# A hybrid recurrence block on one Trainium2 core: w_out by seven products of halves, and the first layer norm's gamma and beta on turned tokens

## The chip, the cores and the metric

The kernel runs on one core of one Trainium2 chip. TensorE (PE) multiplies and transposes into PSUM, VectorE (DVE) and ScalarE (ACT) work on tiles of SBUF and PSUM, GpSimd (POOL) does small things, and SyncE (SP), ScalarE and GpSimd each have a queue on which they issue DMAs. The metric is the device time of one execution in microseconds (us), the median of several runs.

## The reference

One decoder block over 1024 tokens with 1024 channels, all float32:

```
proj = x @ w_in  -> q, f, i, og, pool_v, gate_a, gate_b      (each 1024 wide)
o = HGRN2(q, f, i)                  # gated recurrence, 8 heads of 128
a = rmsnorm_per_head(o) * g * sigmoid(og) @ w_a
b = (causal_mean(pool_v) - pool_v) @ w_pool * pool_scale     # 4 groups, windows 2, 4, 8, 16
mix = (sigmoid(gate_a) * a + sigmoid(gate_b) * b) @ w_out
x = LN1(alpha * x + mix)            # gain ln1_g, bias ln1_b
x = LN2(alpha * x + relu(x @ w_up)^2 @ w_down)               # hidden width 4096
```

## The kernel before

**Products in three parts.** A float32 operand is split into a high half (rounded to the fp32r format, a cast on ScalarE) and a low half (operand minus high half, a subtraction on VectorE). One 128-deep step of a product is three matmuls of 128x512: high by high, high by low, low by high. A tile with two halves of 512 columns comes from the pool `act`; the parts of a weight tile come from the ring `w` (`w_part`, L256 and L257; `NW` = 10 tiles, so five pairs).

**Products by halves.** Most large products (w_in, w_a, w_up, w_down) are already done by seven products of halves in place of eight: tokens and weights are each cut into four quarters a11, a12, a21, a22 and b11 ... b22, sums of quarters are formed (on tokens s1 ... s4, on weights t1 ... t4), and seven products of such quarters are added up with signs. `pair` writes the seven out for two columns of blocks, `prod` (L219, L221, L222) issues one of them: four 128-deep steps, twelve matmuls. Its results leave PSUM by a copy on ScalarE (L303) and additions on VectorE (L307). The product by w_out alone is done whole: `mix(t, cc)` takes a row of 128 tokens and 512 columns and runs `mm3` (L114 to L116) over eight steps, 24 matmuls, in 16 such groups.

**Order.** A scheduler places each engine's instructions by the priority of the code's order and its own clock; `tc.high_priority` and `tc.issue_after` bend it. Nothing overtakes on an engine or a DMA queue at run time.

**The stretch in question.** Around 640 us the products by w_a end; `gated` multiplies by the gates (`ga`, from DRAM) and adds the pooled branch (`gb`), and the result is split and kept as `merged[u][j]` (u: half of the tokens, j: block of 128 channels). Then come the w_out groups. After each, `scalar_tensor_tensor` adds alpha times the residual into the row tile `r[t]` (L1390), `bn_stats` takes the statistics, and after a row's second half `layer_norm` runs: a square root on ScalarE (L1339), an Identity with scale and bias (L1350), a product by gamma on VectorE (L1351) and an addition of beta on POOL (L1352); rows 6 and 7 do it all on VectorE in halves. The finished row goes to DRAM (`xd`, issued on SP) for the second residual, and is transposed on TensorE into turned tokens (channels on partitions), rows 0 to 3 by `first_tokens` (a11, a12) and rows 4 to 7 by `second_tokens` (s3 and a22; s2, s1, s4 follow from them). When the left halves of rows 4 to 7 have been transposed, blocks of w_up for the third pair of units are loaded into their tiles (`r<-in_w_up_dram`, SP). `units(i, raw)` is one pair of blocks of the up stage, i from 0 to 15: product by w_up, Relu, Square (L1434, L1435), sums, and stores of hidden tiles (`put`).

**Pools.** All tiles of SBUF come from rings; an operation that wants a tile of a ring waits until the one that it replaces has been read. `act` has 28, `rows` 8, `c` (from `ca`, `wq` and, in the up stage, `up`) 4, 2 and 4.

## Time and profile before

| | us |
|---|---|
| median of 3 runs (lowest, highest) | 1435.21 (1435.06, 1435.75) |
| the profiled execution | 1434.66 |
| its span, from first to last instruction | 1433.0 |
| TensorE busy | 1420.8 |
| VectorE busy | 1099.2 |
| ScalarE busy | 753.2 |
| POOL busy | 110.9 |

The mean granted TensorE clock was 0.999 of full speed. A busy share is an average over stages with different limits, and matmuls overlap each other, so that the distance from one's start to the next one's start says what it costs. In a row of a timeline, the last bracket is the engine's idle time before the instruction and what ended it.

### The profile page before, as it was taken

How to read it: one execution, taken by the hardware profiler on the slowest of the kernel's cores; microseconds unless marked ns; L12 is line 12 of the kernel's file. 1: busy time of each engine (PE TensorE's matmuls, PEld its weight loads, DVE VectorE, ACT ScalarE, POOL GpSimd, SP SyncE). 2: the span in 40 equal slices, each digit the busy share in tenths (PEclk: the TensorE clock that was granted, in tenths of full speed). 3: DMA queues.
4: the chain of work that ended last, by engine and by line, in shares of the span. 5: the costliest groups of instructions: out<-in, count | busy, mean ns of one | idle time of the engine just before them, and what ended most of it. 6: DMA issues, size and time to landing. Idle time of an engine off the chain costs nothing.

```text
span 1433.0 us, 21208 instructions
## 1 busy us (share of the span) xinstructions
PE 1420.8 (99%) x7499; PEld 1180.1 (82%) x7499; DVE 1099.2 (77%) x1832; ACT 753.2 (53%) x1376; POOL 110.9 (8%) x300
## 2 busy tenths in 40 slices
PE   9999999999999999999999999999999999999997
PEld 7888888888888888878888888888888888888886
DVE  6967887897797796679965697666666887777978
ACT  5445566566656656455522376555556433433534
POOL 0002011111212110100003000000000100000000
PEclk9999999999999999999999999999999999999999
DMA  7142254444444546899551315444457864444422
GB/s 272 60 140 89 90 131 148 126 115 150 113 118 133 150 123 190 237 322 340 182 198 74 103 59 188 153 159 161 162 177 243 299 235 146 150 151 157 132 74 118
DMA packets 187179, 228.18 MB, mean 159 GB/s; under 512 B 12576, under 2 KB 111168, under 8 KB 187072
## 3 DMA queue, kind: packets, MB, share of 16 engines
q1 hardware_dynamic: 180464, 210.94, 44.6%
q0 software_dynamic: 5824, 13.63, 4.7%
q10 hardware_dynamic: 784, 2.25, 0.5%
q8 instruction: 59, 0.97, 0.3%
q14 instruction: 48, 0.39, 0.1%
HBM read 149.70 MB, written 77.07 MB: 158 GB/s over the span
## 4 chain that ended last, share of the span: by engine, by line
PE 95%; DVE 2%; DMA 1%; ACT 1%; issue 1%; POOL 0%; DVEq 0%; ACTq 0%; SPq 0%; POOLq 0%
PE ps_pj L219 16%; PE ps_pj L222 16%; PE ps_pj L221 16%; PE ps_pj L1565 4%; PE ps_pj L1566 4%; PE ps_pj L1564 4%; PE ps_pj L115 2%; PE ps_pj L114 2%; PE ps_pj L116 2%; PE ps_tr L1566 2%; PE ps_tr L1565 2%; PE ps_tr L1564 2%; PE ps_hg L219 1%; PE ps_sc L219 1%; PE ps_sc L222 1%; PE ps_hg L221 1%
## 5 line engine op out<-in xcount | busy, mean ns | idle before, releaser
L219 PE MATMUL ps_pj<-act,w 128*128 128x512 f32 x1068 | 419.9, 393 | 0.3 <-ACT c L303 0.2
L222 PE MATMUL ps_pj<-act,w 128*128 128x512 f32 x1068 | 415.3, 390 | 0.0
L221 PE MATMUL ps_pj<-act,w 128*128 128x512 f32 x1068 | 415.3, 389 | 0.0
L256 ACT CAST w<-raw 128x512 fp32r<-128x512 f32 x303 | 187.7, 621 | 255.4 <-PE ps_pj L221 169.7
L257 DVE TENSOR_TENSOR w<-raw,w 128x512 fp32r<-128x512 f32 x303 | 207.2, 686 | 93.6 <-ACT w L256 92.3
L219 PEld LDWEIGHTS ps_pj<-act,w 128*128 128x128 f32 x1068 | 200.5, 188 | 44.1 <-ACT c L303 1.3
L222 PEld LDWEIGHTS ps_pj<-act,w 128*128 128x128 f32 x1068 | 200.5, 188 | 42.4
L221 PEld LDWEIGHTS ps_pj<-act,w 128*128 128x128 f32 x1068 | 200.6, 188 | 40.5
L1526 ACT CAST act<-act 128x1024 fp32r<-128x1024 f32 x66 | 67.0, 1050 | 108.2 <-issue 35.0
L1527 DVE TENSOR_TENSOR act<-act,act 128x1024 fp32r<-128x1024 f32 x66 | 79.4, 1220 | 18.1 <-ACT act L1526 18.1
L1566 PE MATMUL ps_pj<-act,act 128*128 128x512 f32 x240 | 93.0, 389 | 0.0
L1565 PE MATMUL ps_pj<-act,act 128*128 128x512 f32 x240 | 93.0, 389 | 0.0
L1564 PE MATMUL ps_pj<-act,act 128*128 128x512 f32 x240 | 92.5, 389 | 0.0
L307 DVE TENSOR_TENSOR c<-c,ps_pj 128x512 f32<-128x512 f32 x91 | 62.1, 682 | 32.5 <-PE ps_pj L222 31.8
L303 ACT COPY c<-ps_pj 128x512 f32<-128x512 f32 x92 | 53.3, 581 | 3.0 <-PE ps_pj L222 1.9
L1564 PEld LDWEIGHTS ps_pj<-act,act 128*128 128x128 f32 x240 | 45.0, 188 | 9.4
L1565 PEld LDWEIGHTS ps_pj<-act,act 128*128 128x128 f32 x240 | 45.0, 188 | 9.4
L1566 PEld LDWEIGHTS ps_pj<-act,act 128*128 128x128 f32 x240 | 45.0, 188 | 9.3
L312 DVE TENSOR_TENSOR raw<-raw,raw 128x512 f32<-128x512 f32 x43 | 29.6, 689 | 25.5 <-DMA raw<-in_w_in_dram 16.1
L1435 ACT ACTIVATE c<-c 128x512 f32<-128x512 f32 x61 | 38.5, 632 | 1.7
L1434 ACT ACTIVATE c<-c 128x512 f32<-128x512 f32 x46 | 29.0, 632 | 16.4 <-DVE c L307 16.4
L751 POOL DMA_DIRECT2D s<-og x28 | 24.9, 1161 | 133.2 <-DVE og L1177 133.2
(433 smaller groups left out, 2684.6 us busy)
## 6 DMA issues: line engine op xcount, KB each, us to landing
h<-c SPq DMA_DIRECT2D x106, 256.0 KB, 3.0
raw<-in_w_in_dram SPq DMA_DIRECT2D x100, 256.0 KB, 3.3
act<-h SPq DMA_DIRECT2D x78, 256.0 KB, 3.0
draw<-in_w_down_dram SPq DMA_DIRECT2D x16, 1024.0 KB, 8.2
raw<-in_w_up_dram SPq DMA_DIRECT2D x56, 256.0 KB, 2.9
hf<-h SPq DMA_DIRECT2D x34, 256.0 KB, 3.0
s<-og POOLq DMA_DIRECT2D x28, 256.0 KB, 6.4
v<-v SPq DMA_DIRECT2D x16, 256.0 KB, 3.5
```

The source lines that it names most:

```text
L219: PE.matmul(ps, wh[:, k], th, start=first and k == 0, stop=False, skip_group_check=True)
L221: PE.matmul(ps, wh[:, k], tl, start=False, stop=False, skip_group_check=True)
L222: PE.matmul(ps, wl[:, k], th, start=False, stop=k == CH - 1, skip_group_check=True)
L256: hi_of.append(A.copy(hi, src).ins)
L257: lo_of.append(V.tensor_sub(lo, src, f(hi)).ins)
L303: noted(A.copy(t, ps))
L307: last_add[0] = V.tensor_add(t, t, ps).ins
L1526: A.copy(hi, src)
L1527: V.tensor_sub(lo, src, f(hi))
L1564: PE.matmul(ps, hh[:, w], wh, start=fresh and n == 0, stop=False, skip_group_check=True)
L1565: PE.matmul(ps, hh[:, w], wl, start=False, stop=False, skip_group_check=True)
L1566: PE.matmul(ps, hl[:, w], wh, start=False, stop=n == M - 1, skip_group_check=True)
```

## The change

**The w_out product** becomes seven products of quarters, by `out_product`: p1, p2, p6, p5, p3, p7, p4, each of four groups of twelve matmuls, which go on in two chains of four PSUM banks. Each product's result is added into the rows by `scalar_tensor_tensor` as it comes. The sums of w_out's quarters (t1 to t4) are formed early, before the recurrence, by `out_sums`: loads into tiles that the recurrence uses later, four operations on VectorE for each k, and stores to DRAM on POOL's queue. The operands are split when they are needed: `split_tokens` for the gated rows, `split_rows` (loads on POOL's queue into `c` tiles) for the weights.

**The first layer norm.** Rows 0 to 3 get their sums from `accum_out` and a Square on ScalarE, rows 4 to 7 keep `bn_stats`. `norm_row` writes only the normalised row, without gain and bias, and stores it (`nd`). Gain and bias go on behind the transposes, where they are one number per partition: in `first_normed` for rows 0 to 3, and by an Identity in `second_tokens(normal=True)` for rows 4 to 7. `prm` holds them; two more small loads are issued on ScalarE's queue at the start.

**The residual rows** with gain and bias, for the second layer norm, are made in the up stage, one row after each of `units` 5 to 12: `residual_row` loads `nd` on POOL's queue into one of three `y` tiles, does four operations on VectorE, and stores `xd` on POOL's queue. The pool for w_down's blocks (`fw`) opens later for it.

```diff
+        def out_sums(k, queue, *tags):
+            rooms = [tt(tag) for tag in tags]
+            for t, (kh, nh) in zip(rooms, ((0, 1), (1, 1), (0, 0), (1, 0))):
+                queue.dma_start(out=t, in_=out_rows_of(kh, nh)[k])
+            b12, b22, b11, b21 = rooms
+            V.tensor_sub(b22, b22, b12)
+            V.tensor_sub(b12, b12, b11)
+            V.tensor_add(b11, b22, b11)
+            V.tensor_sub(b21, b21, b11)
+            for name, t in (("t3", b22), ("t1", b12), ("t2", b11), ("t4", b21)):
+                nc.gpsimd.dma_start(out=out_td[name][k], in_=t)
...
+        for k in range(CH):
+            out_sums(k, nc.gpsimd if k > 1 else nc.sync, *(("tA", "tA", "tE", "tD") if k % 2 else ("tH", "tH", "st", "st")))
...
+        def split_tokens(srcs):
+            return [split_act(t) for t in srcs]
+
+        def split_rows(srcs, tile_of):
+            made = []
+            for src in srcs:
+                t, (hi, lo) = c_tile(), tile_of()
+                nc.gpsimd.dma_start(out=t, in_=src)
+                A.copy(hi, t)
+                V.tensor_sub(lo, t, f(hi))
+                made.append((hi, lo))
+            return made
...
+    def out_product(name, chain, fresh, u, nh, whole, then=None):
...
+            ps, w = chains[chain][c], slice(c * P, (c + 1) * P)
+            for k, ((xh, xl), (wh, wl)) in enumerate(zip(xs, ws)):
+                PE.matmul(ps, xh[:, w], wh, start=fresh and k == 0, stop=False, skip_group_check=True)
+                PE.matmul(ps, xh[:, w], wl, start=False, stop=False, skip_group_check=True)
+                PE.matmul(ps, xl[:, w], wh, start=False, stop=k == CH - 1, skip_group_check=True)
...
+            with tc.high_priority(PRIO):
+                if whole and u:
+                    V.scalar_tensor_tensor(y, y, scale, ps, ALU.mult, ALU.add)
+                    V.bn_stats(parts_of_row[t][:, nh], y)
...
+        for i in range(2 if t == 7 else 1):
+            w = slice(i * HALF, (i + 1) * HALF) if t == 7 else slice(0, D)
+            A.activation(y[:, w], y[:, w], AF.Identity, bias=mv[:, 2:3], scale=mv[:, 3:4])
+            nc.sync.dma_start(out=nd[t][:, w], in_=y[:, w])
...
+    out_product("p1", 1, True, 0, 0, False)
+    out_ops["p2"].insert(0, split_tokens(tokens(0, 1)))
+    out_ops["p6"] = split_tokens(s2), split_rows(out_td["t2"], row_parts)
+    out_product("p2", 0, True, 0, 0, True)
...
+    out_product("p3", 1, False, 0, 1, True, norm_row)
+    out_ops["p4"] = split_tokens(tokens(1, 1)), split_rows(out_td["t4"], act_parts)
+    out_product("p7", 0, True, 1, 1, True)
+    xt[:] = [r[c][:, HALF:] for c in range(CH)], [c_tile() for _ in range(CH)], [r[c][:, :HALF] for c in range(CH)]
+    first_normed("a12", "pj")
+    first_normed("a11", "pj")
+    out_product("p4", 0, False, 1, 0, True, norm_row)
...
+                if normal:
+                    t = s[kp] if name == "s3" else half_act()
+                    normed(t, ps, kp + CH * (name == "a22"))
+                    ps = t
...
+        def residual_row(t):
+            y = res.tile([P, D], F32, tag="y", name=nm("y"), bufs=3)
+            nc.gpsimd.dma_start(out=y, in_=nd[t])
+            for i in range(2):
+                w = slice(i * HALF, (i + 1) * HALF)
+                V.tensor_mul(y[:, w], y[:, w], g1[:, w])
+                V.tensor_add(y[:, w], y[:, w], b1[:, w])
+            nc.gpsimd.dma_start(out=xd[t], in_=y)
...
             run(units(i, raw))
+            if 0 <= i - 5 < 8:
+                residual_row(i - 5)
```

Where the instructions stand shows in the built order. First, ScalarE at the turn from the w_out stage into the up stage, before. The first two rows are the statistics of rows 6 and 7 (r_1639 and r_1644, which VectorE normalises); r_1629 is the tile of row 4, and the cast from it takes a block of w_up that has been loaded there:

```order
L1339 ACTIVATE lmv_1643_8771<-lmv_1643_8771,eps_ln_88 128x1
L1339 ACTIVATE lmv_1648_8837<-lmv_1648_8837,eps_ln_88 128x1
L256 CAST w_1671_8940<-raw_1654_8860 128x512
L256 CAST w_1675_8959<-raw_1655_8862 128x512
L256 CAST w_1678_8977<-raw_1651_8855 128x512
L303 COPY c_1662_8898<-ps_pj_1661_8885 128x512
L256 CAST w_1681_8983<-raw_1680_8981 128x512
L1434 ACTIVATE c_1662_8898<-c_1662_8898 128x512
L256 CAST w_1695_9059<-r_1629_8582 128x512
L132 CAST act_1664_8906<-r_1593_8246 128x512
```

The same place after, with r_1620, r_1622, r_1624 and r_1626 the tiles of rows 4, 5, 6 and 7, L1443 the Identity of `norm_row`, L273 what was L256:

```order
L1443 ACTIVATE r_1620_8461<-r_1620_8461,lmv_1688_8907 128x1024
L1438 ACTIVATE lmv_1689_8928<-lmv_1689_8928,eps_ln_88 128x1
L273 CAST w_1724_9119<-raw_1723_9117 128x512
L1438 ACTIVATE lmv_1690_8949<-lmv_1690_8949,eps_ln_88 128x1
L273 CAST w_1740_9201<-r_1620_8461 128x512
L320 COPY c_1705_9030<-ps_pj_1704_9017 128x512
L1443 ACTIVATE r_1622_8477<-r_1622_8477,lmv_1689_8928 128x1024
L1438 ACTIVATE lmv_1691_8970<-lmv_1691_8970,eps_ln_88 128x1
L1443 ACTIVATE r_1624_8493<-r_1624_8493,lmv_1690_8949 128x1024
L1501 ACTIVATE c_1705_9030<-c_1705_9030 128x512
L1443 ACTIVATE r_1626_8509<-r_1626_8509,lmv_1691_8970 128x512 x2
```

The cast from row 4's tile stood behind the normalisation of all eight rows; now it stands behind row 4's and ahead of that of rows 5, 6 and 7. Second, TensorE at the same place, before (r_1629, r_1634, r_1639, r_1644 are rows 4 to 7):

```order
L222 MATMUL ps_pj_1661_8885<-act_1620_8542,w_1660_8882 128x512
L177 MATMUL ps_tr_1663_8900<-ident_74,r_1629_8582 128x128
L177 MATMUL ps_tr_1663_8900<-ident_74,r_1634_8648 128x128
L177 MATMUL ps_tr_1663_8900<-ident_74,r_1639_8714 128x128
L177 MATMUL ps_hg_1665_8909<-ident_74,r_1629_8582 128x128
```

and after, from the last transposes of row 5 on:

```order
L177 MATMUL ps_tr_1710_9052<-ident_74,r_1622_8477 128x128
L177 MATMUL ps_sc_1712_9062<-ident_74,r_1622_8477 128x128
L177 MATMUL ps_tr_1706_9032<-ident_74,r_1624_8493 128x128
L177 MATMUL ps_hg_1708_9042<-ident_74,r_1624_8493 128x128
L177 MATMUL ps_tr_1710_9052<-ident_74,r_1624_8493 128x128
L177 MATMUL ps_sc_1712_9062<-ident_74,r_1624_8493 128x128
L177 MATMUL ps_tr_1706_9032<-ident_74,r_1626_8509 128x128
L177 MATMUL ps_hg_1708_9042<-ident_74,r_1626_8509 128x128
L177 MATMUL ps_tr_1710_9052<-ident_74,r_1626_8509 128x128
L177 MATMUL ps_sc_1712_9062<-ident_74,r_1626_8509 128x128
L236 MATMUL ps_pj_1716_9080<-act_1681_8862,w_1714_9076 128x512
```

Before, three rows are transposed together, and the fourth behind them. After, the transposes go row by row: row 4's four, then twelve products less four that stand between them, then rows 5, 6 and 7, and behind these 24 products by parts (w_1714 first) that are made earlier. Third, VectorE in the up stage, where before the parts of w_up and the additions follow each other:

```order
L257 TENSOR_TENSOR w_1796_9647<-raw_1786_9604,w_1795_9646 128x512
L257 TENSOR_TENSOR w_1799_9665<-raw_1785_9603,w_1798_9664 128x512
L344 TENSOR_TENSOR raw_1785_9603<-raw_1787_9606,raw_1786_9604 128x512
L307 TENSOR_TENSOR c_1772_9524<-c_1772_9524,ps_pj_1761_9452 128x512
L257 TENSOR_TENSOR w_1803_9688<-raw_1785_9603,w_1802_9687 128x512
```

and after, where y_1886, y_1916 and y_1946 are the first three residual rows, and L274 is what was L257:

```order
L274 TENSOR_TENSOR w_1838_9772<-raw_1829_9745,w_1837_9771 128x512
L1566 TENSOR_TENSOR y_1886_10063<-y_1886_10063,ln_1797_9579 128x512 x2
L354 TENSOR_TENSOR raw_1829_9745<-raw_1829_9745,raw_1831_9748 128x512
L1567 TENSOR_TENSOR y_1886_10063<-y_1886_10063,ln_1798_9581 128x512 x2
L324 TENSOR_TENSOR c_1817_9668<-c_1817_9668,ps_pj_1806_9596 128x512
L274 TENSOR_TENSOR w_1841_9791<-raw_1831_9748,w_1840_9790 128x512
L1566 TENSOR_TENSOR y_1916_10230<-y_1916_10230,ln_1797_9579 128x512 x2
L274 TENSOR_TENSOR w_1844_9809<-raw_1830_9747,w_1843_9808 128x512
L1567 TENSOR_TENSOR y_1916_10230<-y_1916_10230,ln_1798_9581 128x512
L1566 TENSOR_TENSOR y_1946_10397<-y_1946_10397,ln_1797_9579 128x512
```

The code asks for a residual row after each of units 5 to 12; in the order all eight stand in one run of 66 operations, of which 32 are theirs, from the parts of unit 4 on.

217 lines of the change are left out of this document (113 added, 104 removed).

## The prediction

> **What bounds the kernel now.** I read the page first, then the waits of TensorE, then its timeline for the pitch of the products, then sums by stretch around the place of the change, and last the single rows there. The page's head, its chain and the waits of TensorE (engine, line, for whom, us in total, times, longest):
>
> ```profile
> span 1433.0 us, 21208 instructions
> PE 1420.8 (99%) x7499; PEld 1180.1 (82%) x7499; DVE 1099.2 (77%) x1832; ACT 753.2 (53%) x1376; POOL 110.9 (8%) x300
> PE 95%; DVE 2%; DMA 1%; ACT 1%; issue 1%; POOL 0%; DVEq 0%; ACTq 0%; SPq 0%; POOLq 0%
> PE ps_hg L480 <- POOL ident masks.py:199: 1.8, 1, 1.8
> PE ps_tr L114 <- DVE f L905: 1.4, 1, 1.4
> PE ps_tr L177 <- DVE x L204: 0.7, 1, 0.7
> PE ps_sc L538 <- DVE c L580: 0.5, 1, 0.5
> PE ps_pj L219 <- ACT c L303: 0.2, 1, 0.2
> ```
>
> TensorE carries 95% of the chain and waits 4.6 us in all (1.8 + 1.4 + 0.7 + 0.5 + 0.2). So two things alone move the time: fewer products, or a new wait on TensorE. Taking work off another engine earns nothing. What a product is worth comes from the timeline (start, length, engine, line), in the middle of the w_out stage:
>
> ```profile
> 760.16 0.39 PE L115 MATMUL ps_pj<-w,act 128*128 128x512 f32 x1
> 760.39 0.39 PE L116 MATMUL ps_pj<-w,act 128*128 128x512 f32 x1
> 760.62 0.39 PE L114 MATMUL ps_pj<-act,act 128*128 128x512 f32 x1
> 760.84 0.39 PE L115 MATMUL ps_pj<-act,act 128*128 128x512 f32 x1
> ```
>
> Each row is 0.39 us long, but starts come 0.227 us apart (three steps in 0.68): the pitch is the price, not the length. Now the sums by stretch (us from:to, length, busy us of PE, PEld, DVE, ACT, POOL, clock):
>
> ```profile
> 100.00:120.00 20.00, 20.00 (x90) 16.57 (x89) 12.34 (x19) 10.12 (x18) 0.00 (x0) 1.00 0.26 80
> 640.00:710.00 70.00, 70.00 (x310) 57.96 (x309) 67.75 (x112) 41.13 (x75) 0.00 (x0) 1.00 0.84 277
> 720.00:810.00 90.00, 90.00 (x414) 74.60 (x414) 52.90 (x91) 27.60 (x45) 14.39 (x6) 1.00 0.32 116
> 820.00:830.00 10.00, 10.00 (x49) 8.27 (x49) 9.27 (x17) 6.35 (x12) 0.00 (x0) 1.00 0.44 134
> 830.00:870.00 40.00, 39.78 (x180) 32.69 (x179) 40.00 (x68) 29.36 (x53) 0.00 (x0) 1.00 0.34 114
> 900.00:1000.00 100.00, 100.00 (x443) 82.81 (x442) 61.83 (x95) 56.66 (x96) 0.00 (x0) 1.00 0.46 156
> ```
>
> VectorE is packed ahead of the w_out stage (67.75 of 70), half idle within it (52.90 of 90), and without a gap from 830 to 870, in the first units of the up stage. There TensorE keeps running by a hair. The change puts work into the idle part, and its end touches the packed part.
>
> **1. Fewer products.** Out go 16 groups of 24 products (384); in come seven of 48 (336). 48 x 0.227 = 10.9 us of TensorE. The rest of TensorE's list is as long as before: 6149 rows become 6101. Term: -10.9.
>
> **2. VectorE inside the w_out stage.** Its unit price is the step between back-to-back operations:
>
> ```profile
> 842.01 2.49 DVE L206 TENSOR_TENSOR c<-r,c 128x512 f32<-128x512 f32 x4
> 844.42 1.28 DVE L257 TENSOR_TENSOR w<-raw,w 128x512 fp32r<-128x512 f32 x2
> L1351 DVE TENSOR_TENSOR r<-r,act 128x1024 f32<-128x1024 f32 x6 | 7.4, 1226 | 7.0 <-ACT r L1350 7.0
> ```
>
> Four in 2.41 us: 0.60 each. The stage gets 24 more low halves (56 for 32), 12 more additions into the rows (28 for 16) and 16 sums of token tiles, and loses 8 bn_stats: 44 x 0.60 = 26.4. The six gamma products (7.4) go. That is +19.0, and idle are 90 - 52.90 = 37.1, less the 10.9 by which the stage shrinks: some 7 us are left over. What VectorE loses by standing behind a late load must fit in there. Where it has always work it is idle 3% (640 to 710) to 7% (820 to 830): 2.5 to 5.8 of 79 us, both under 7. Each product's operands are needed one by one, so I take +0.5, with 0 to 5 as bounds (5 if it idles 15%, 12 us).
>
> **3. The turn into the up stage.** Here a wait is added, and it is the dearest item. Before, rows 4 to 7 are all normalised before any engine waits for the w_up block that is loaded into their left halves:
>
> ```profile
> 818.37 0.49 PE L177 MATMUL ps_sc<-ident,r 128*128 128x128 f32 x3
> 821.88 0.62 ACT L256 CAST w<-r 128x512 fp32r<-128x512 f32 x1 [1.57 <-DMA r<-in_w_up_dram]
> 822.40 0.62 ACT L132 CAST act<-r 128x512 fp32r<-128x512 f32 x1
> 822.93 0.63 ACT L1435 ACTIVATE c<-c 128x512 f32<-128x512 f32 x1
> 823.46 0.57 ACT L303 COPY c<-ps_pj 128x512 f32<-128x512 f32 x1
> 823.92 1.66 ACT L132 CAST act<-r 128x512 fp32r<-128x512 f32 x3
> L1350 ACT ACTIVATE r<-r,lmv 128x1024 f32<-128x1024 f32 x6 | 7.5, 1246 | 2.5 <-DVE lmv L1349 2.5
> r<-in_w_up_dram SPq DMA_DIRECT2D x4, 256.0 KB, 3.8
> x<-r SPq DMA_DIRECT2D x7, 512.0 KB, 2.6
> ```
>
> From the end of the transposes that free the tile (818.37 + 0.49) to the cast that waited for the load are 3.0 us; the wait is ScalarE's alone and TensorE runs on. In the new order the same cast (of row 4's tile) stands on ScalarE ahead of the normalisation of rows 5, 6 and 7, whose transposes stand on TensorE ahead of 24 products that are ready. So TensorE waits for: the load (3.0), the cast (0.52, by the starts above), a copy (0.46), row 5 (1.2), row 6 (1.2), two small square roots (0.2 together), a Relu (0.53) and the halves of row 7 (1.06): 8.2. It has 8 products left to do in that time, 1.8 us. Term: +6.4. Low end 2 (the load lands while ScalarE is still at the statistics of these rows, and the four normalisations alone are late); high end 9.8 (the store of row 4 must land first, 2.6 us, and the load takes its 3.8). I take 6.4, by the row that is the same load into the same tile.
>
> The Trainium skill, DMA: Bandwidth & Descriptors, section "Anatomy of one DMA", fits 2.0 us plus bytes over 436 GB/s, an estimate of 2.6 us for these 256 KB, for transfers issued from GpSimd; by it the wait would be 6.0 and the time 0.4 lower. This case's row, 3.8 on SP's queue, says rather longer.
>
> **4. Gamma and beta on turned tokens.** Eight Identity operations on ScalarE take the place of eight copies; eight more (0.53 each) stand before the s3 and a22 operands, in the packed stretch, where TensorE's wait at L219 was 0.2. Most of them run while TensorE works on a11 and a12: +0.3, bounds 0 and 4.2 (all eight in the way).
>
> **5. The sums of w_out before the recurrence.** 16 VectorE operations (9.6 us) go into stretches like 100 to 120, idle 7.7 of 20, so there is room for them; but the order puts them ahead of the recurrence's first scan. At worst about half of them, 5 us, push that scan back. Against that:
>
> ```profile
> 132.15 0.75 DVE L1072 TENSOR_TENSOR tC<-tE,ek 128x256 f32<-128x256 f32 x2
> 135.80 0.60 PE L1092 MATMUL ps_tr<-ident,tC 128*128 128x128 f32 x4
> ```
>
> The scan's result is ready at 132.90 and TensorE takes it at 135.80: 2.9 us of cover. +0.3, bounds 0 and 2.1 (5 less 2.9).
>
> **6. Residual rows in the up stage.** 32 operations, 19.2 us, where VectorE is idle 38 of 100. But the order packs all eight rows into one run of 66 operations (39.6 us) that holds 14 low halves of w_up parts; one such part feeds 12 products, so TensorE needs 14 x 12 x 0.227 = 38.1 us for them. The three y tiles go round: a tile's store and the next load must land before the fourth row.
>
> ```profile
> act<-x POOLq DMA_DIRECT2D x7, 512.0 KB, 7.2
> s<-og POOLq DMA_DIRECT2D x28, 256.0 KB, 6.4
> s<-og SPq DMA_DIRECT2D x16, 256.0 KB, 2.5
> c<-o POOLq DMA_DIRECT2D x8, 256.0 KB, 5.3
> ```
>
> A turn is 6.4 + 7.2 = 13.6 us by these, against 14 operations (8.4) between the first row's end and the fourth's start: 5.2 of standing; later rows add 1.0 and 1.8. With the 1.5 by which 39.6 exceeds 38.1, VectorE falls 9.5 behind. The parts run ahead by up to four pairs of w tiles, 4 x 12 x 0.227 = 10.9, or by three PSUM banks, 8.2. So 0 to 1.3: +0.5; if the cover is gone, up to 4.
>
> The two loads that ScalarE issues more at the start lie beside TensorE's longest wait, for POOL: nothing. POOL's six additions (14.39 us) go, off the path: nothing.
>
> **The sum.** -10.9 + 0.5 + 6.4 + 0.3 + 0.3 + 0.5 = -2.9. The profiled execution took 1434.66 us (its span and 1.7 around it), so 1431.8; the median of the three runs was 1435.21, 0.55 above it, so 1432.3. 0.2% is 2.9 us, about what a measurement of this kernel can tell from no change; the forecast lies on that line.
>
> **Rivals.**
> A: the wait at the turn is covered (the load lands before ScalarE gets to it, VectorE being the later). Then -10.9 and about 1.6 of small terms: 1425.9; 1424.3 if those vanish too. For it: TensorE hid all of this before. Against: the order of the three normalisations behind the cast.
> B, slower: ScalarE becomes the engine of the turn. Its place is the stretch from row 4's transposes to the a22 products. To the 9.8 of part 3's high end come the eight Identity operations, 4.2: 14.0 us, so -10.9 + 14.0 + 1.3 = +4.4, 1439.6. It decides slower once these waits pass 12.5 us (-10.9 + 12.5 + 1.3 = 2.9). For it: no slack from 830 to 870. Against: ScalarE was busy only 29.36 of 40 there.
> C: the transfers that moved to POOL's queue come late. The row for s<-og is 6.4 there against 2.5 on SP's, though those on POOL's add up in DRAM. VectorE then idles 15% in the w_out stage (+5.0) and the ring costs 1.3: -10.9 + 5.0 + 6.4 + 0.6 + 1.3 = +2.4, 1437.6. The Trainium skill, SBUF — State Buffer, section "SBUF: two separate sides", has a rule that speaks for it: while VectorE runs operations in a two-port mode, GpSimd cannot write the descriptors of its DMAs. No run here shows POOL's queue stopped beside a packed VectorE.
> D: a product is worth its length, 48 x 0.39 = 18.7 in place of 10.9: 1424.5. The starts speak against it.
>
> **Chances.** Forecast 0.40 (half of it beyond 0.2% faster, 0.19 within, 0.01 slower); A 0.24 and D 0.02, faster; B 0.22, slower; C 0.12, half within 0.2%, half slower. Faster 0.20 + 0.24 + 0.02 = 0.46; same 0.19 + 0.06 = 0.25; slower 0.01 + 0.22 + 0.06 = 0.29. The forecast's own range is 1428.5 to 1435.5. The range for 8 in 10 goes from A's low end to a little past B, 1424 to 1441.
>
> **What would show it.** In the new profile: products still 0.227 apart; a wait on TensorE for the row normalisation of rows 5 to 7, about 6.4 us, and before it an idle ScalarE released by the load into row 4's tile; no wait longer than 1 us at the residual rows or the first scans. The forecast is wrong if that wait is under 2 or over 10 us, or if TensorE waits inside the seven products for low halves or additions.

## The result and the profile after

| | before | changed |
|---|---|---|
| median of 4 runs, us (lowest, highest) | 1435.37 (1435.06, 1435.75) | 1445.01 (1441.68, 1446.73) |
| the profiled execution | 1434.66 | 1445.29 |

The ratio is 1.0064, with a 95% interval of 1.0046 to 1.0083. The change made the kernel slower by 9.6 us, where 2.9 us faster was forecast, and the time lies outside the range. The head of the page of the changed kernel, with its chain:

```profile
span 1443.6 us, 21398 instructions
PE 1417.4 (98%) x7451; PEld 1172.9 (81%) x7451; DVE 1141.1 (79%) x1928; ACT 772.2 (53%) x1411; POOL 133.8 (9%) x362
PE 86%; DMA 6%; DVE 4%; ACT 2%; issue 1%; SPq 0%; DVEq 0%; ACTq 0%
```

The 48 matmuls are gone (7499 to 7451), but TensorE's share of the chain fell from 95% to 86%: the chain now runs through transfers, VectorE and ScalarE. The longest waits of TensorE after the change (for whom, us in total, times, longest):

```profile
PE ps_tr L177 <- ACT r L1443: 3.6, 2, 2.9
PE ps_sc L236 <- ACT c L320: 2.3, 1, 2.3
PE ps_hg L499 <- POOL ident masks.py:199: 1.8, 1, 1.8
```

The third is the old one. By this view all waits of TensorE come to 17.7 us, for 4.6 before, and the first two rows are two places.

**The turn into the up stage.** ScalarE there (start, length, line, last bracket: idle before and who ended it):

```profile
814.41 0.62 ACT L273 CAST w<-r 128x512 fp32r<-128x512 f32 x1 [3.52 <-DMA r<-in_w_up_dram]
814.93 0.58 ACT L320 COPY c<-ps_pj 128x512 f32<-128x512 f32 x1
815.41 1.24 ACT L1443 ACTIVATE r<-r,lmv 128x1024 f32<-128x1024 f32 x1
816.74 1.23 ACT L1443 ACTIVATE r<-r,lmv 128x1024 f32<-128x1024 f32 x1
818.39 1.51 ACT L1443 ACTIVATE r<-r,lmv 128x512 f32<-128x512 f32 x2
```

TensorE in the same stretch:

```profile
811.19 0.27 PE L177 MATMUL ps_tr<-ident,r 128*128 128x128 f32 x1
816.70 0.33 PE L177 MATMUL ps_tr<-ident,r 128*128 128x128 f32 x1 [2.94 <-ACT r L1443]
818.02 0.47 PE L177 MATMUL ps_tr<-ident,r 128*128 128x128 f32 x1 [0.66 <-ACT r L1443]
820.01 0.78 PE L236 MATMUL ps_pj<-act,w 128*128 128x512 f32 x1
820.59 0.63 PE L238 MATMUL ps_pj<-act,w 128*128 128x512 f32 x1
821.01 0.63 PE L239 MATMUL ps_pj<-act,w 128*128 128x512 f32 x1
```

Row 4's last transpose ends at 811.46; the cast that waits for the block loaded into its tile starts 2.95 us later; the normalisations of rows 5 to 7 stand behind it, and TensorE behind them. The products that follow start 0.42 us apart in place of 0.227. That is the second cost at this place, and the granted clock shows it (us from:to, length, busy of PE, PEld, DVE, ACT, POOL, clock, DMA share, GB/s):

```profile
818.00:820.00 2.00, 1.87 (x8) 1.47 (x9) 0.00 (x0) 2.00 (x4) 0.00 (x0) 0.50 0.99 395
820.00:822.00 2.00, 2.00 (x7) 1.61 (x6) 0.88 (x2) 2.00 (x4) 0.00 (x0) 0.50 0.77 236
822.00:824.00 2.00, 2.00 (x7) 1.52 (x5) 2.00 (x4) 2.00 (x4) 0.00 (x0) 0.50 1.00 339
824.00:826.00 2.00, 2.00 (x9) 1.64 (x8) 2.00 (x4) 1.66 (x4) 0.00 (x0) 0.91 0.80 235
856.00:858.00 2.00, 2.00 (x6) 1.58 (x5) 2.00 (x4) 0.59 (x1) 0.00 (x0) 0.50 0.32 111
```

For six us behind the wait TensorE runs at half its clock, and in 822 to 824 it is "busy" for 2.00 us with 7 products instead of 9: a busy share does not show this loss, the clock column does. The last row is of the second place.

**A second wait, near 852 us.** TensorE's rows, and below them ScalarE's:

```profile
852.22 0.40 PE L238 MATMUL ps_pj<-act,w 128*128 128x512 f32 x1
854.97 0.72 PE L236 MATMUL ps_sc<-act,w 128*128 128x512 f32 x1 [2.35 <-ACT c L320]
```

```profile
849.13 1.66 ACT L132 CAST act<-c 128x512 fp32r<-128x512 f32 x3
853.31 1.13 ACT L1502 ACTIVATE c<-c 128x512 f32<-128x512 f32 x2
854.35 0.56 ACT L320 COPY c<-ps_sc 128x512 f32<-128x512 f32 x1
```

TensorE wants a PSUM bank that ScalarE copies out at 854.35, behind casts of s4 and Relu units. 0.7 us are lost just before it at 851, and the clock is at 0.50 again behind it (856 to 858, above). The same stretches by sums:

```profile
790.00:810.00 20.00, 20.00 (x106) 16.74 (x105) 15.88 (x31) 10.53 (x16) 0.00 (x0) 1.00 0.29 113
810.00:830.00 20.00, 16.10 (x68) 12.33 (x67) 14.50 (x31) 14.00 (x24) 0.00 (x0) 0.83 0.44 150
830.00:860.00 30.00, 27.11 (x116) 21.75 (x115) 30.00 (x51) 22.54 (x42) 0.00 (x0) 0.94 0.22 70
860.00:880.00 20.00, 20.00 (x90) 16.57 (x89) 12.61 (x20) 11.97 (x22) 0.00 (x0) 1.00 0.48 170
```

VectorE stands 5.5 of 20 us at the turn, most of it in one piece, and is then full for 30 us without a gap:

```profile
821.12 1.35 DVE L221 TENSOR_TENSOR r<-r 128x512 f32<-128x512 f32 x2 [3.84 <-ACT r L197]
```

In the kernel before it was as full (40.00 of 40), and TensorE ran on.

**Where the 10.6 us between the profiled executions come from.** TensorE's lists differ by the 48 matmuls of the w_out stage alone. So the same place can be found in two profiles by counting matmuls, from the first one up to that stage and from the last one behind it, and the difference of the two starts says what has been lost (plus) or won (minus) up to there. In us, against the kernel before; e6, e9, e12 and e15 are experiments of the next section:

| start before, us | stretch that ends there | changed | e6 | e12 | e15 | e9 |
|---|---|---|---|---|---|---|
| 87.9 | the start | -0.2 | -0.2 | +0.3 | 0.0 | +0.5 |
| 188.3 | the head | +2.1 | +2.4 | +0.4 | +5.3 | +0.5 |
| 434.0 | recurrence | +2.0 | +2.5 | +0.5 | +5.4 | +0.6 |
| 512.3 | recurrence, near 490 | +4.1 | +3.6 | +4.5 | +9.4 | +4.9 |
| 638.9 | up to the products by w_a | +4.3 | +3.5 | +5.3 | +8.7 | +4.1 |
| 684.2 | products by w_a | +6.2 | +5.4 | +5.3 | +10.3 | +4.1 |
| 752.0 | w_out, 48 matmuls fewer | -4.7 | -5.4 | -5.6 | -0.6 | -6.8 |
| 827.4 | the turn | +3.0 | -5.5 | -5.6 | -0.4 | -6.8 |
| 872.3 | the second wait | +7.5 | +1.5 | -0.5 | +3.0 | -6.8 |
| 915.4 | the residual rows | +10.1 | +3.7 | -0.5 | +5.1 | -6.8 |
| 1425.2 | the rest | +10.2 | +4.7 | -0.3 | +5.4 | -6.5 |

In the changed kernel the w_out stage wins 10.9 us. The turn costs 7.7: 4.5 of standing (3.11 + 0.70 + 0.36 + 0.31), and most of the rest is half clock (nine products, 1.8, and eight transposes 0.21 us apart for 0.11). The second place costs 4.5 (3.5 of standing and seven slow steps, 1.4, less 0.4 that the kernel before lost there), the residual rows 2.6, the head 2.3, the recurrence near 490 2.1, the products by w_a 1.9. Behind the start of the last matmul 0.4 more are lost.

### The profile page after: what moved, and what is told of

Read it like the earlier page. It is cut to its first block, busy times and chain, and to the rows that moved or that the text cites. A ratio compares the mean times of both kernels' runs of the same rounds, so it can differ in the third digit from the quotient of the medians.

```text
span 1443.6 us, 21398 instructions
## 1 busy us (share of the span) xinstructions
PE 1417.4 (98%) x7451; PEld 1172.9 (81%) x7451; DVE 1141.1 (79%) x1928; ACT 772.2 (53%) x1411; POOL 133.8 (9%) x362
## 4 chain that ended last, share of the span: by engine, by line
PE 86%; DMA 6%; DVE 4%; ACT 2%; issue 1%; SPq 0%; DVEq 0%; ACTq 0%
PE ps_pj L236 15%; PE ps_pj L238 14%; PE ps_pj L239 14%; PE ps_pj L1649 4%; PE ps_pj L1650 4%; PE ps_pj L1648 4%; PE ps_tr L1649 2%; PE ps_tr L1650 2%; PE ps_tr L1648 2%; DMA act<-in_w_in_dram 1%; DMA raw<-in_w_a_dram 1%; PE ps_hg L236 1%; PE ps_hg L239 1%; PE ps_sc L236 1%; PE ps_hg L238 1%
## 5 line engine op out<-in xcount | busy, mean ns | idle before, releaser
L273 ACT CAST w<-raw 128x512 fp32r<-128x512 f32 x303 | 187.2, 621 | 239.7 <-PE ps_pj L238 172.4
L274 DVE TENSOR_TENSOR w<-raw,w 128x512 fp32r<-128x512 f32 x303 | 206.8, 686 | 78.7 <-ACT w L273 77.3
L320 ACT COPY c<-ps_pj 128x512 f32<-128x512 f32 x92 | 53.5, 581 | 4.6 <-DMA v<-c 3.6
```

What stands on the lines that cost most here:

```text
L273: hi_of.append(A.copy(hi, src).ins)
L274: lo_of.append(V.tensor_sub(lo, src, f(hi)).ins)
L320: noted(A.copy(t, ps))
```

## The experiments

Each timed kernel ran on one chip with the kernel before, so the ratio to that is what compares; the changed kernel's is 1.0064 [1.0046, 1.0083].

| run | median, us | ratio, 95% interval |
|---|---|---|
| e1_free_products | 1445.43 | 1.0075 [1.0057, 1.0093] |
| e2_weights_on_sp | 1443.76 | 1.0065 [1.0048, 1.0081] |
| e3_no_sums | 1447.14 | 1.0088 [1.0068, 1.0108] |
| e4_no_residual_rows | 1440.25 | 1.0040 [1.0027, 1.0054] |
| e5_clock_kept | 1447.16 | 1.0076 [1.0053, 1.0099] |
| e6_less_statistics | 1439.94 | 1.0024 [1.0011, 1.0037] |
| e7_48_more | 1451.90 | 1.0107 [1.0087, 1.0127] |
| e8_all_loads_on_sp | 1441.38 | 1.0038 [1.0026, 1.0050] |
| e9_before_48_less | 1428.28 | 0.9942 [0.9926, 0.9958] |
| e10_no_late_gain | 1445.62 | 1.0069 [1.0052, 1.0085] |
| e11_two_mended | 1438.59 | 1.0019 [1.0009, 1.0030] |
| e12_costs_off | 1431.80 | 0.9970 [0.9958, 0.9982] |
| e13_less_vector | 1444.95 | 1.0060 [1.0047, 1.0072] |
| e14_less_scalar | 1445.80 | 1.0061 [1.0049, 1.0073] |
| e15_less_both | 1436.32 | 0.9993 [0.9984, 1.0003] |
| e16_gpsimd_sums | 1443.97 | 1.0052 [1.0040, 1.0064] |
| e17_order_all | 1451.42 | 1.0099 [1.0083, 1.0114] |
| e18_order_light | 1445.29 | 1.0063 [1.0049, 1.0077] |

The intervals of e4 and e8 still overlap the changed kernel's a little, so their gains are less sure than those of e6, e11, e12 and e15.

**Is the turn's wait a matter of order? (e1, e5)** e1 lets the 24 ready products stand ahead of the transposes that wait:

```diff
-        with tc.issue_after(turned[1]):
-            run(pairs[1][:1])
-        with tc.issue_after(turned[3]):
-            run(pairs[1][1:2])
+        run(pairs[1][:1])
+        run(pairs[1][1:2])
```

> The two constraints that hold the second pair's products on a12 and a11 behind the transposes of rows 4 to 7 are taken away; in the order 24 ready products then stand ahead of the transposes of rows 5 to 7, and nothing else of the work changes. Theory (a wait at the turn, then a halved clock): the changed kernel's gaps at 812 to 818 us (4.2 us) and the 7 us at a granted clock of 0.50 behind them (3.6 us lost) go, and half of the second gap near 852 with its slow stretch may go with them: 7 to 10 us faster than the changed kernel's 1445, so 1435 to 1438. Rival (VectorE is the bound of this stretch, so the gap only moves): the s3 operands come 2 to 6 us late right behind the transposes, the clock falls there instead, and the time stays at 1443 to 1446.

The wait at the turn is gone, and the time is the changed kernel's. The sums by stretch of e1, 15 us later:

```profile
830.00:832.00 2.00, 1.06 (x6) 0.51 (x4) 2.00 (x4) 2.00 (x5) 0.00 (x0) 1.00 0.00 0
832.00:834.00 2.00, 0.63 (x1) 0.19 (x1) 2.00 (x5) 2.00 (x5) 0.00 (x0) 0.79 0.00 0
834.00:836.00 2.00, 1.17 (x3) 0.98 (x4) 2.00 (x5) 2.00 (x5) 0.00 (x0) 0.50 0.06 13
```

VectorE and ScalarE are both full (2.00 and 2.00 of 2), and TensorE stands there, with the clock drop behind it. e5 keeps the clock up instead, by 26 transposes more while TensorE waits:

```diff
-    def transposed(tiles, off, kp, tag):
+    def transposed(tiles, off, kp, tag, idle=0):
...
+            for _ in range(idle if c == 1 else 0):
+                PE.transpose(ps[:, P : 2 * P], tiles[0][:, off + kp * P : off + (kp + 1) * P], ident)
...
+                    (..., 26 if (name, kp) == ("s3", 0) else 0)
```

> 26 more transposes of row 4 are written to where row 5's will stand (overwritten by it), between row 4's and row 5's transposes: work without use that TensorE does while it waits at the turn. Theory (the idle gap is what halves the clock): the gap falls under 1.5 us, the granted clock stays 1.00 at 818 to 824, and the steps of 0.427 us there vanish. If TensorE is the bound behind the turn, that is worth 2.5 to 3.6 us (1441.5). Rival (VectorE is the bound from 815 to 870, so a faster TensorE waits longer at the next gap): the clock stays up, but the gap near 852 grows by about as much, and the time stays within 1 us of the changed kernel's.

The clock stays at 1.00 there and the wait sinks to 1.61 us, but waits of 1.1 us at 837, 2.3 at 852 and 1.3 at 932 follow, and the time does not fall. Both say the same: filling TensorE's wait at the turn earns nothing here, since about as much is lost behind it. That the other two engines' work is what holds the stretch is argued from their full rows.

**Loads on GpSimd's queue (e2, e4, e8).** The wait at 682 us, seen from VectorE of the changed kernel, and the loads of that time (KB each, median us to landing), the last row being that of the kernel before:

```profile
679.46 0.69 DVE L329 TENSOR_TENSOR raw<-raw,raw 128x512 f32<-128x512 f32 x1 [2.49 <-DMA raw<-in_w_a_dram]
682.56 0.69 DVE L329 TENSOR_TENSOR raw<-raw,raw 128x512 f32<-128x512 f32 x1 [2.41 <-DMA raw<-in_w_a_dram]
c<-in_w_out_dram POOLq DMA_DIRECT2D x6, 256.0 KB, 6.1
raw<-in_w_a_dram SPq DMA_DIRECT2D x1, 512.0 KB, 9.4
```

```profile
raw<-in_w_a_dram SPq DMA_DIRECT2D x1, 512.0 KB, 6.2
```

On GpSimd's queue the loads of w_out no longer stand behind those of w_a, but run beside them, and the last block of w_a lands after 9.4 us in place of 6.2. e2 puts the w_out blocks on SyncE's queue:

```diff
-                nc.gpsimd.dma_start(out=t, in_=src)
+                nc.sync.dma_start(out=t, in_=src)
```

> The loads of w_out's parts for the seven products are issued on SP's queue in place of POOL's; TensorE's order is the same. Theory (transfers on a second queue run beside those in front on SP's, so the w_a blocks that VectorE waits for land late): the 512 KB load of w_a near 670 us lands in about 6 us in place of 9.4, the gap near 682 (1.5 us) goes, 1.5 us faster than the changed kernel. Rival (the DMA engines are full there whatever the queue, so the same bytes are only sorted otherwise and the weights come late to the products): the gap near 682 stays or a gap in the w_out stage takes its place, and the time is the same or up to 3 us more.

The wait at 682 is gone; in time nothing shows. e4 leaves the residual rows out:

```diff
-            if 0 <= i - 5 < 8:
-                residual_row(i - 5)
...
-                nc.gpsimd.dma_start(out=r[t], in_=xd[t])
+                nc.gpsimd.dma_start(out=r[t], in_=nd[t])
```

> Leaves out the residual rows' gain and bias in the up stage (8 loads, 32 VectorE operations, 8 stores); the second residual reads the normalised rows without them, so the output is not the reference's. Theory (their first loads, 512 KB each on POOL's queue, delay a block of w_up near 887 us): the gap near 891 (1.7 us) and the small ones near 910 (0.7) go, 2.4 us faster than the changed kernel. Rival (VectorE's bunch is what costs): gaps from 900 to 940 go and the one near 891 stays.

The waits at 891 and 910 are gone, and the ratio is 0.0024 lower (about 3.4 us). e8 makes the edit of e2 and puts the loads of the residual rows on SyncE's queue as well (`nc.sync.dma_start(out=y, in_=nd[t])`):

> The loads of w_out's parts and the loads of the residual rows are issued on SP's queue in place of POOL's; nothing is left out. Theory (a second queue lets later transfers run beside the ones in front): the gaps near 682 and near 891 go, 2.5 to 4 us less than the changed kernel's, 1441 to 1442.5. Rival (the residual rows' bytes cost whatever the queue): the gap near 891 stays and the time is that of the run with the weights alone on SP's queue, 1443 to 1444.

The waits at 682 and 891 are both gone, the ratio is 0.0026 lower. It is the fastest of the kernels that leave nothing out, and slower than before all the same.

**The sums at the head, the gain at the turn (e3, e10).** e3 leaves `out_sums` out and loads w_out's quarters in place of the sums; e10 leaves the Identity of `second_tokens` out (the last two lines):

```diff
-        for k in range(CH):
+        for k in range(0):
             out_sums(k, nc.gpsimd if k > 1 else nc.sync, ...
...
+    out_td = {name: out_rows_of(kh, nh) for name, kh, nh in (("t1", 0, 1), ("t2", 1, 1), ("t3", 0, 0), ("t4", 1, 0))}
...
-                    second_tokens(name, tag, normal=True)
+                    second_tokens(name, tag)
```

> Leaves out the sums of w_out's quarters (16 loads, 16 VectorE operations, 16 stores before the recurrence); the products read quarters of w_out in their place, so the output is not the reference's. Theory (their transfers hold up the loads of w_in and v around 97 us): the gaps at 97, 101 and 137 us, 1.9 us together, go and nothing else moves: 1443. Rival (the later gaps near 487 and 494, 2.3 us, come from the recurrence being pushed back at its head): these go too, 1440.5 to 1441.

> Leaves out gain and bias of the turned tokens of rows 4 to 7 (8 Identity operations on ScalarE between transposes and operands), so the output is not the reference's. Theory (the second gap near 852 is ScalarE's and VectorE's packed row behind the transposes, lengthened by these eight): the second gap falls from 3.2 to under 1.5 us and its slow clock goes; 3 to 5 us less than the changed kernel's 1445. Rival (the second gap comes of the order in which copies out of PSUM stand behind Relus on ScalarE): it stays at 2.5 to 3.5 us, and the time moves by less than 2 us.

Without the sums the 1.9 us of waits near 97, 101 and 137 us go, and the time does not, against both forecasts: in that profile waits of 2.3 us at 930 and 1.2 at 846 stand against it. The waits near 486 and 493 us stay as well, so they do not come from the sums. e10's second wait is 0.65 + 2.0 us, and its time the changed kernel's.

**Early statistics for rows 4 to 7 (e6).** The statistics of the left halves of these rows are left out, so that the normalisation is early:

```diff
-                    V.bn_stats(parts_of_row[t][:, nh], y)
+                    if nh:
+                        V.bn_stats(parts_of_row[t][:, nh], y)
```

> Rows 4 to 7 take their statistics from their right halves alone, known before the product p4 (4 bn_stats of 0.6 us less on VectorE at the turn, and nothing between the last addition and the normalisation), so the output is not the reference's. Theory (VectorE's and ScalarE's row of work at the turn is the bound): the gap at the turn falls from 4.2 us to under 2, the clock does not fall, the second gap shrinks by 1 to 2 us: 1437 to 1440. Rival (the load of w_up into row 4's tile ahead of rows 5 to 7 on ScalarE is the bound): the gap stays at 3 to 4 us, since the load can start no earlier than row 4's transposes, and the time is within 1.5 us of the changed kernel's.

Sums of e6 at the turn and at the second wait:

```profile
810.00:820.00 10.00, 10.00 (x56) 8.34 (x54) 6.74 (x11) 7.33 (x14) 0.00 (x0) 1.00 0.41 118
840.00:850.00 10.00, 5.84 (x21) 3.73 (x20) 10.00 (x18) 7.40 (x14) 0.00 (x0) 0.96 0.23 70
```

TensorE is busy without a break at the turn, at full clock, and the ratio falls by 0.0040 (5.7 us). The second wait remains (2.77 + 1.2 + 0.6 us), and by the table of starts the second place now costs 7.0 us in place of 4.5: a part of what is won at the turn is lost there. e6 changes more than the amount: in its built order all four normalisations (L1444, from 798.96 to 808.75) stand ahead of the cast from row 4's tile (815.80). What that order alone is worth is for e17 to say.

**The worth of 48 products (e7, e9).** e7 does p7 of w_out twice (48 matmuls more); e9 is the kernel before with two of eight steps left out in the groups of rows 0 to 3 (48 matmuls less):

```diff
-            for k, ((xh, xl), (wh, wl)) in enumerate(zip(xs, ws)):
+            for k, ((xh, xl), (wh, wl)) in list(enumerate(zip(xs, ws))) * (1 + (name == "p7")):
...
-for k in (0, 1, 2, 3, 4, 6, 5, 7)
+for k in ((0, 1, 2, 3, 4, 6) if t < CH else (0, 1, 2, 3, 4, 6, 5, 7))
```

> The product p7 is done twice, the second time over the first: TensorE has the 48 products back (10.9 us at 0.227), nothing else changes. If TensorE is the bound in the w_out stage and at the turn, the time is 10.9 us longer than the changed kernel's, 1456. If VectorE and ScalarE set the pace up to the turn, the gaps there (4.2 us, 3.6 by the halved clock, 3.2 and 2.1 at the second) are filled by the additional products in good part, and the time is only 0 to 5 us longer, 1445 to 1450.

> The kernel before with 48 products left out: the groups of rows 0 to 3 run six of their eight steps, so the output is not the reference's; all loads, splits and the old layer norm stay. Theory (TensorE is the bound of the old arrangement, a product is worth its pitch of 0.227 us): 10.9 us faster than before, 1424 to 1425. Rival (VectorE or ScalarE follows so closely at the turn that shorter products only uncover them): a gap opens near 820 and the gain is under 6 us.

In the changed kernel 48 products more cost 0.43% by the ratios, 6.2 us in place of 10.9, between the two forecasts: in e7's profile the turn costs 0.7 us for 7.7, since they fill the wait there, and the second place 8.1 for 4.5. In the kernel before 48 fewer bring 0.58%, 8.3 us, again between the forecasts, and 11 in its best run (1424.30). The table of starts says where the rest went in the profiled execution: e9 wins the full 10.9 in the w_out stage (+4.1 to -6.8) and keeps it through the turn and the stretch behind it, but it had lost 4.3 near 490 us, in the recurrence, ahead of its edit. That loss comes and goes: the profile of the kernel before lacks it, e2 and e13 have next to none of it, e9 and e12 have 4. So with the old instructions at the turn a saving of this size arrives whole, and the 2.1 us of the changed kernel near 490 need not be the change's.

**Several costs at once (e11, e12).** e11 joins the edits of e6 and e8; e12 joins those of e2, e3, e4, e6 and e10.

> Two changes together: all loads of w_out's parts and of residual rows on SP's queue, and the statistics of rows 4 to 7 from their right halves alone (the output differs from the reference's by that). If the costs are separate, they add: 3.6 and 5.1 us less than the changed kernel's 1445, 1436 to 1437, still no better than before. If both shorten the same chain, 1439 to 1441.

> Left out together: the sums of w_out's quarters, the residual rows, gain and bias of the late tokens, half the statistics of rows 4 to 7; the loads of w_out's parts go on SP's queue. The output is not the reference's. The seven products, their splits and their additions stay. Theory (each of these costs a wait, the products themselves save 10.9 us): 1426 to 1430, 5 to 9 us faster than before. Rival (the splits and additions of the seven products on VectorE cost the gain by themselves): 1433 or more.

e11 comes to 1.0019, between its two forecasts: it gains 0.0045, where the gains of e6 and e8 add up to 0.0066. e12, with the sums, the residual rows, half of the statistics and the late gain left out, is 0.30% faster than before, 4.2 us of 10.9, and lies between its forecasts too. In the table of starts its head, w_a, turn and residual rows cost next to nothing; what stays is the loss in the recurrence and the second place, 5.1 us, with waits of 0.7, 0.7 and 1.7 us near 845.

**The second wait: VectorE, ScalarE, or the order? (e13, e14, e15, e17, e18)** e13 leaves out eight subtractions on VectorE (the low parts of s1 and s4), e14 the squares on ScalarE, e15 joins e13 and e6:

```diff
+            if normal and name in ("s1", "s4"):
+                no_low.add(name)
+                xp[name][kp] = act_tile()
+                hi = A.copy(xp[name][kp][:, 0], (a11 if name == "s1" else a12)[kp]).ins
...
-            A.activation(t, t, AF.Square)
```

> The changed kernel without the eight low parts of the turned tokens of s1 and s4 at the head of the up stage (their two products take the high part twice, so as many products run; part of the computation is left out). That takes 8 instructions of 0.60 us, 4.8 us, from VectorE between 840 and 857 us. If VectorE, which stands still nowhere between 830 and 860 us there, is what makes the second wait (0.7 + 2.5 us near 850 and 2 us at half the clock behind it), that wait goes or sinks under 1 us, the turn's 4 us stay, and the time falls by 4 to 6 us, to 1439 to 1441. If it is the order of ScalarE's copies behind its casts, the casts stay, the wait stays over 2 us and the time at 1444 to 1446.

> The changed kernel with the squares left out of the up stage (Relu alone; part of the computation is left out), which takes 0.53 us a unit from ScalarE ahead of the copies that release TensorE at 855 us, and nothing from VectorE in the stretch 830 to 857 us. If ScalarE's queue makes the second wait, it falls by 1 us or more and the time by 2 to 4 us; if VectorE does, the wait stays at 2 to 3 us, and the time falls by less than 1.5 us.

> The low parts of s1 and s4 left out as well as the statistics of the left halves of rows 4 to 7 (part of the computation is left out): 2.8 and 4.8 us less on VectorE in the stretch from 800 to 857 us. If VectorE bounds this stretch, both places are without waits over 1 us and without half clock, and the time is 1435 to 1437: 9 us below the changed kernel. If not, the second wait stays as it did with the statistics alone, 1439 to 1441.

e13 gave the time of the other theory (1.0060). Its rows at the wait, VectorE's and TensorE's (L282 is what L274 was, L328 what L320 was):

```profile
848.03 0.69 DVE L282 TENSOR_TENSOR w<-raw,w 128x512 fp32r<-128x512 f32 x1 [1.91 <-ACT w L281]
848.53 0.69 PE L244 MATMUL ps_pj<-act,w 128*128 128x512 f32 x1 [2.91 <-ACT c L328]
```

VectorE now waits itself, 1.91 us for a cast of ScalarE, which stood behind seven casts of tokens. So 4.8 us less on VectorE do not take the wait away. Less on ScalarE does not either, though e14 takes little from ahead of the copy at 854.35 (two squares, about 1.1 us): it still waits 2.48 us there, at 1.0061. With both edits of e15, the two places look like this:

```profile
836.00:838.00 2.00, 1.14 (x4) 0.60 (x4) 2.00 (x5) 2.00 (x5) 0.00 (x0) 1.00 0.54 160
846.00:848.00 2.00, 0.97 (x4) 0.49 (x4) 2.00 (x4) 1.98 (x4) 0.00 (x0) 1.00 0.00 0
850.00:852.00 2.00, 1.13 (x6) 0.65 (x5) 1.25 (x2) 2.00 (x5) 0.00 (x0) 1.00 0.34 103
```

The long wait is broken into pieces of about 1 us (0.8, 1.2, 1.0), the clock stays at 1.00, the second place costs 3.4 us by the table of starts, for 7.0 in e6, and the ratio is 0.9993. The time is the one forecast for it: 0.7% below the changed kernel, with some 7 us of VectorE's work (12 operations of 0.60) taken out between the end of w_out and 857 us. e17 and e18 leave the amount and change the order, on ScalarE: the casts of s4 behind a copy of c (both), rows 5 to 7 ahead of the cast that waits for its load (e17), beside the loads on SyncE's queue (both) and e6's edit (e18):

```diff
-                with tc.issue_after(made_last[after]) if after else nullcontext():
+                with tc.issue_after(made_last[after]) if after else nullcontext(), behind_act() if name == "s4" else nullcontext():
```

> Nothing left out; the orders alone are changed: on ScalarE the normalisations of rows 5 to 7 stand ahead of the cast of w_up that waits for its load, the casts of s4 stand behind the copy of c for p6 in the up stage, and the block and residual loads are on SyncE's queue. If the orders of ScalarE make the two waits, the turn falls from 3.6 us to about 2 and the second wait from 2.5 to under 1 us, both with less half clock: 1436 to 1438, against 1441.4 with the loads on SyncE's queue alone. If the chain of both engines' work makes them, the waits move to the next product, and the time stays at 1440 to 1443.

> The statistics of the left halves of rows 4 to 7 left out (part of the computation), the block and residual loads on SyncE's queue, and the casts of s4 behind the copy of c for p6: beside the 1438.6 of the same kernel without the last. If the order of the casts of s4 against the copies makes the second wait, it falls from 2.6 us to under 1 us and the time to 1434 to 1436, under the time before; if not, it is 1438 to 1440.

At the turn e17 does what it was to do (the wait falls from 3.1 to 2.0 us), but the turn still costs 6.2 us by the starts, for 7.7: the normalisations now stand behind a copy for which ScalarE waits 2.92 us on TensorE. So the load in front of rows 5 to 7 explains a part of the turn, and e6's gain there needs the early statistics too. The second wait does not sink; the longest waits of e17's TensorE:

```profile
PE ps_pj L236 <- ACT c L320: 4.8, 1, 4.8
PE ps_pj L239 <- DVE w L274: 3.6, 1, 3.6
```

With s4 later, the order puts other products ahead that are not ready, and it costs 0.61% against e8 (e17) and 0.44% against e11 (e18), which have no such order. Both runs miss both of their forecasts. What is shown is that none of these three edits alone, less on VectorE, a little less on ScalarE or this order, takes the second wait away, and that work taken out of the whole stretch from w_out's end to 857 us makes it smaller. A late VectorE is not the cause: in e12 the turn costs nothing, VectorE begins the differences for s4 (L225) at 841.9, where the kernel before began them at 848.6, and the place still costs 5.1 us; in e9, with the old instructions, it begins them at 841.7 and nothing is lost. What is left as its cause are the new instructions of this stretch and their order. Which link of the chain through both engines (sum on VectorE, cast on ScalarE, subtraction on VectorE, copy on ScalarE) sets it stays open.

**An idle engine for the sums (e16).** It has e8's loads as well.

```diff
-                V.tensor_add(a11[kp], s[kp], a11[kp])
+                (G if normal else V).tensor_add(a11[kp], s[kp], a11[kp])
...
-                V.tensor_sub(a12[kp], a12[kp], s[kp])
+                (G if normal else V).tensor_sub(a12[kp], a12[kp], s[kp])
```

> Nothing left out: the eight sums and differences that make s1 and s4 of the up stage go from VectorE to GpSimd, which has no compute there, and the block and residual loads from GpSimd's queue to SyncE's. VectorE loses 8 x 0.60 = 4.8 us between 840 and 857 us. If GpSimd takes under 1.2 us for one, the second wait goes and the time is 4 us under the 1441.4 that the loads on SyncE's queue alone gave: 1437; if it takes 2 us or more, or VectorE slows down beside it, s1 and s4 come late, the wait moves to their products, and the time is 1442 to 1448.

GpSimd's first two rows, and VectorE's where it first stood still:

```profile
830.43 10.04 POOL L223 TENSOR_TENSOR r<-r 128x512 f32<-128x512 f32 x1 [194.06 <-DVE r L228]
840.44 1.29 POOL L225 TENSOR_TENSOR c<-c,r 128x512 f32<-128x512 f32 x1
841.16 1.12 DVE L133 TENSOR_TENSOR act<-r,act 128x512 fp32r<-128x512 f32 x1 [1.84 <-ACT act L132]
```

One operation takes 1.3 to 1.7 us of GpSimd, but the first took 10.04: it ended at 840.47, 1.15 us after the full VectorE first paused (839.32). TensorE then waits 7.9 us in one piece. It is no way to lighten VectorE here.

## Why the prediction was wrong

The step that failed is the end of the sum: behind the turn it has no term but part 4's +0.3, although the prediction itself had found that stretch, 830 to 870, to be without a gap on VectorE, with TensorE running "by a hair". The runs show 4.5 us lost there in the changed kernel, and 5.1 and 7.0 in e12 and e6, whose turn costs nothing. Smaller misses come on top: the head 2.3 for 0.3, the residual rows 2.6 for 0.5, the products by w_a 1.9 for nothing, the turn 7.7 for 6.4, and 2.1 in the recurrence that come and go.

**1. Fewer products, -10.9.** Right, in pitch (0.227 in both profiles), count and worth: the w_out stage wins 10.9 us in every profile of the table, and e9 keeps it to the end.

**2. VectorE in the w_out stage, +0.5.** Right for the time: between the last product by w_a (682) and the turn (812) TensorE loses nothing. VectorE is fuller than was reckoned, though: 78.82 of 90 us from 720 to 810, where 52.90 + 19.0 would be 71.9. Among what the list left out are eight operations of `first_normed` (0.79 us each) that write the turned tokens on VectorE; a copy on ScalarE did that before. Part 4 misread the same edit: its Identity operations for rows 0 to 3 take the place of casts, not of copies.

**3. The turn, +6.4.** The mechanism and its parts were right: 2.95 us from the transposes to the cast (3.0 forecast), 8.55 from there to the 24 products (8.2 forecast). The load is not all of it, though: with the load out of the way of rows 5 to 7, the turn still costs 6.2 us (e17). The transposes themselves run in the 8.55 us, so the standing is 4.5 and not 6.4. What the term left out is the half clock behind it, most of the other 3.2. The two errors are of opposite sign, and that 7.7 came so near to 6.4 is partly luck. The Trainium skill, *TensorE: Matmul & The Clock Gate*, section "Part 1: The HAM clock gate", has a rule that speaks against the change: after an idle window of some 3.4 us the matrix engine drops to half its clock, and it takes about as long a busy one to come back. With the forecast's own wait of 6.4 us it would have added 1.7 us or more, half of such a window, an estimate from that page. The trace agrees with the drop, and differs in the times: here waits of 2.3 to 3.1 us were mostly enough, and the clock stayed at 0.50 for six us behind one of them (818 to 824).

**What was late next.** The prediction saw "no slack from 830 to 870" and used it against rival B only ("ScalarE was busy only 29.36 of 40 there"). A full VectorE alone costs nothing: e9 comes to this stretch 6.8 us early with the old instructions and loses nothing in it. But the change also puts other instructions and another order there, and for these the sum has nothing. Rival B had the right sign with another mechanism: the wait at the turn never came near its 12.5 us.

**4. Gain and bias, +0.3.** Small, as forecast (e10: no gain in time without them).

**5. The sums at the head, +0.3.** The waits there are 1.9 us, inside the bounds (0 to 2.1) and not at the value taken. Only 0.6 of them (137.8) are the scan that the prediction had in mind; the one near 98 stands behind a copy for which ScalarE had waited 1.71 us for a transfer (`v<-c`), the one near 102 behind a cast. So that their sum lies within the bounds is luck. They go with the sums (e3), which shows no gain in time.

**6. Residual rows, +0.5.** Mis-sized: 2.6 us in the profile (2.0 of it waits), and 0.24% in e4. The order of VectorE was read rightly, but the wait is for a block of w_up, beside which two `y` loads ran on GpSimd's queue (VectorE of the changed kernel there):

```profile
890.15 0.69 DVE L329 TENSOR_TENSOR raw<-raw,raw 128x512 f32<-128x512 f32 x1 [4.22 <-DMA raw<-in_w_up_dram]
```

That is rival C's kind of transfer, the other way round. C had the transfers on GpSimd's queue come late; what came late were those on SyncE's queue next to them, at w_a (1.9 us) and here. e8 prices both at 0.26%.

**The sum.** The two conditions that were to make the forecast wrong did not arise (a wait of 4.5 us lies within 2 to 10, and nothing waits inside the seven products). One of its other signs failed: TensorE waits 1.7 us at the residual rows, where none was to be over 1 us. So the working was right where it looked closest, and left out three things: the clock, the stretch behind the turn, and two transfers.

## What to carry to other kernels

A saving on the critical engine arrives whole if what lies behind it keeps up, as in e9, even through a stretch in which another engine has no gap. When a change also puts other instructions into such a stretch, give the stretch a term of its own. Price a wait of TensorE over 2 us with the slow steps behind it, and look for them in the clock column, since the busy share does not show them. A wait that can be filled by reordering isn't yet time won: here the waits moved until work was taken away. And to see what was won and lost at each place, set the starts of the same matmul in two profiles side by side.

## What the runs showed of the hardware

The half clock was not expected here. Waits of 2.3 to 3.1 us were mostly followed by 2 to 6 us of steps at 0.427 us (in e3 two of 2.3 and 2.5 were not), single waits of 1.2 to 2.0 us mostly not; several short ones together were enough. The sums of e9, whose waits near 485 us are 0.8, 1.6 and 0.3 us:

```profile
488.00:490.00 2.00, 1.57 (x19) 1.23 (x20) 1.37 (x3) 2.00 (x10) 0.00 (x0) 0.77 0.67 216
490.00:492.00 2.00, 2.00 (x6) 1.61 (x5) 2.00 (x4) 1.98 (x8) 0.20 (x1) 0.50 1.01 296
```

Six products in two us there, for nine at full clock.

A GpSimd operation with two inputs from SBUF took 10.04 us beside a full VectorE and 1.29 when it came next (e16). The Trainium skill, *SBUF — State Buffer*, section "SBUF: two separate sides", says that the two engines share a pair of ports that one holds for a whole instruction while the other is blocked. The trace agrees, with 10.04 us against 1.29 to 1.73; here the block lasted through a whole run of VectorE instructions.
